# The last layer norm of a two-layer decoder trunk: g taken into the rows as they arrive, and one sum with b - mean * rstd * g

## The chip, the cores and the metric

The kernel runs on one core of one Trainium2 chip. The metric is the device time of one execution in microseconds; three timed runs of the kernel before gave a median of 2086.51 us. Engines are called PE (matmuls), DVE (VectorE), ACT (ScalarE), POOL (GpSimd) and SP (SyncE, which issues the DMAs).

## What is computed

Two post-norm decoder layers over 512 rows of 2048 channels in float32. Only the end of the second matters here: the mixed heads go through an output projection, the residual is added, and the last layer norm follows.

```python
def layer_norm(x, g, b):
    mean = jnp.mean(xf, axis=-1, keepdims=True)
    var = jnp.mean(jnp.square(xf - mean), axis=-1, keepdims=True)
    return ((xf - mean) * lax.rsqrt(var + LN_EPS) * g + b).astype(x.dtype)
...
    return o.astype(x.dtype) @ w_o                       # end of the second layer
...
    x = layer_norm(DEEPNORM_ALPHA * x + y, ln_g[layer], ln_b[layer])
```

## The kernel before, in words

Rows are cut into four slices of 128 rows, t0 to t3, which lie on the 128 partitions; channels run along the free axis. `proj_ln` makes the projection. A weight in float32 is split into a high and a low part (`split`: ACT copies the high part at L137, DVE subtracts at L141), and each product takes three matmuls (L506 to L508). The output columns come in groups: 0 to 511 (for this layer already made, and read back as `y`), 512, 1024, then 1536 to 1791. In these groups the four slices are worked on together. The last group, columns 1792 to 2047, has all its weights resident, so that PE finishes one slice after the other: the statistics of a slice are complete as soon as PE has left it, while PE works on the next.

After each group `evac` adds the residual to the matmul result for one slice (L457, DVE, PSUM and SBUF in, SBUF out, into the row buffer `s`), and takes statistics of 256 columns (L459, BN_STATS). After the last group of a slice DVE merges them (L495), and `rstd` is made of five small instructions: ACT's square root (L209), and L211, L214, L216, L220 on DVE. Then `after` normalizes the slice in `layer1_out`:

- DVE, columns 0 to 1023 (0 to 1791 for t3): `(s - mean) * g` at L1287, and later `s * rstd + b` at L1295, in pieces of 512 columns.
- ACT, POOL, the other columns: ACT makes `s * rstd - mean * rstd` (L1291, with `nmr` from L1289), POOL multiplies by g (L1292) and adds b (L1293).
- SP stores pieces of 512 columns (L1281). The residual pieces are loaded by SP too (L1276), into a pool of six buffers with the tag `xr`.

g and b lie in SBUF as `lng` and `lnb`, broadcast to all partitions; their loads (L1272) are issued ahead of the group that starts at column 1024. The order of the instructions on each engine is set when the program is built; each engine runs its own list in order and waits on semaphores. In the list of DVE the first instruction of a slice (L457) stands behind the last of the slice before.

Of the kernel before, what the change touches and what calls it, by code (L numbers as in the profile page):

```python
# [8 lines left out]
F32 = mybir.dt.float32  # L9
F32R = mybir.dt.float32r  # L10
I32 = mybir.dt.int32
AF = mybir.ActivationFunctionType
ALU = mybir.AluOpType
# [4 lines left out]
P = 128  # L18
S = 512
D = 2048  # L20
NK = D // P
NT = S // P
# [12 lines left out]
class Kernel:  # L35
# [402 lines left out]
                nc.scalar.activation(t, pm, AF.Copy, scale=hs[:, 2 * g + n:2 * g + n + 1])  # L438
                yield t

    def proj_ln(self, ctx, W, mixed, residual, after, first=None, start=None):

        nc, tc = self.nc, self.tc
        rp = ctx.enter_context(tc.tile_pool(name="wres", bufs=1))
        sp = ctx.enter_context(tc.tile_pool(name="lns", bufs=1))
        st = [sp.tile([P, D], F32, name=f"s{t}") for t in range(NT)]
        stats = [sp.tile([P, 8, 6], F32, name=f"st{t}") for t in range(NT)]

        def unit(c0, k0, nk, w, pool=None, bufs=None):
            return self.wunit(W[k0 * P:(k0 + nk) * P, c0:c0 + w].rearrange("(k p) n -> p k n", p=P),
                              nk, w, pool, bufs)

        def evac(t, c0, w, ps):
            sl = st[t][:, c0:c0 + w]
            nc.vector.scalar_tensor_tensor(sl, residual(t, c0, w), ALPHA, ps, ALU.mult, ALU.add)  # L457
            for j in range(c0, c0 + w, 256):
                nc.vector.bn_stats(stats[t][:, j // 256, :], st[t][:, j:j + 256])  # L459

        def mms(ps, t, k, w, kk):
            tk = slice(t * P, (t + 1) * P)
            self.mm3b(ps, mixed[k][:, 0, tk], mixed[k][:, 1, tk], w[0][:, kk, :], w[1][:, kk, :], k == 0, k == NK - 1)

        for c0, wd in ((0, 512), (512, 512), (1024, 512), (1536, 256)):
# [6 lines left out]
            for k0 in range(0, NK, nk):  # L472
                w = unit(c0, k0, nk, wd)
# [15 lines left out]
        for t in range(NT):  # L489
# [6 lines left out]
            rstd = lambda: self.rsqrt_eps(sp, mv[:, 1:2], LN_EPS, 1, f"ln{t}")  # L496
            g = after(t, st[t], mv[:, 0:1], rstd)
# [760 lines left out]
    def layer1_out(self, x1_d, mixed, y_d):  # L1258
        nc, tc, i = self.nc, self.tc, self.i
        with ExitStack() as ctx:  # L1260
            rp = ctx.enter_context(tc.tile_pool(name="res1", bufs=6))
            rp.tile([P, 112], F32, name="pad1", bufs=1)
            wp = ctx.enter_context(tc.tile_pool(name="wp1", bufs=2))
            bv = {}

            def start(c0):

                if c0 == 1024:
                    self.wp, self.ww = wp, 1024
                    for n, ap in (("g1", i["ln_g"][1:2]), ("b1", i["ln_b"][1:2])):  # L1270
                        t = bv[n] = rp.tile([P, D], F32, name="ln" + n, bufs=1)
                        nc.sync.dma_start(t, ap.to_broadcast([P, D]))  # L1272

            def residual(t, c0, w):
                r = rp.tile([P, 512], F32, tag="xr", name="xr")[:, :w]
                nc.sync.dma_start(r, x1_d[t * P:(t + 1) * P, c0:c0 + w])  # L1276
                return r

            def after(t, sf, mean, rstd):
                g, b = bv["g1"], bv["b1"]  # L1280
                out = lambda sl: nc.sync.dma_start(self.out[0, t * P:(t + 1) * P, sl], sf[:, sl])  # L1281
                rstd = rstd()
                cut = 1792 if t == NT - 1 else 1024
                dve = [slice(c, min(c + 512, cut)) for c in range(0, cut, 512)]
                rest = [slice(c, min(c + 512, D)) for c in range(cut, D, 512)]
                for sl in dve:
                    nc.vector.scalar_tensor_tensor(sf[:, sl], sf[:, sl], mean, g[:, sl], ALU.subtract, ALU.mult)  # L1287
                nmr = rp.tile([P, 1], F32, tag="nmr", name="nmr", bufs=2)
                nc.vector.scalar_tensor_tensor(nmr, mean, -1.0, rstd, ALU.mult, ALU.mult)  # L1289
                for sl in rest:  # L1290
                    nc.scalar.activation(sf[:, sl], sf[:, sl], AF.Identity, scale=rstd, bias=nmr)  # L1291
                    nc.gpsimd.tensor_mul(sf[:, sl], sf[:, sl], g[:, sl])  # L1292
                    nc.gpsimd.tensor_add(sf[:, sl], sf[:, sl], b[:, sl])  # L1293
                for sl in dve:
                    nc.vector.scalar_tensor_tensor(sf[:, sl], sf[:, sl], rstd, b[:, sl], ALU.mult, ALU.add)  # L1295
                    out(sl)
                for sl in rest:
                    out(sl)
                yield

            def first(t):
                y = rp.tile([P, 512], F32, tag="y", name="y", bufs=2)
                nc.sync.dma_start(y, y_d[t])
                return y

            self.proj_ln(ctx, i["od_w_o"][0], mixed, residual, after, first, start)


def build(tc, ins, out):
# [26 lines left out]
```

## Time and profile before

| | us |
|---|---|
| three timed runs | 2082.32, 2086.72, 2086.51 (median 2086.51) |
| the profiled execution, its own time | 2082.76 |
| span of its instructions | 2081.1 |
| PE busy | 2015.5 |
| DVE busy | 1281.4 |
| ACT busy | 960.2 |
| POOL busy | 282.9 |

The span is counted from the first instruction to the last; the time of the execution is a little longer. Times in the rows below are microseconds from the span's start. A row names the line of the source, the operation, and the tiles, as output<-inputs.

### The profile page before, as it was taken

What the parts mean: (1) busy time and instruction counts of PE and PEld (TensorE: products, weight loads), DVE (VectorE), ACT (ScalarE), POOL (GpSimd) and SP (SyncE); (2) the same over time, 40 slices, a digit from 0 to 9 for tenths busy, and PEclk for the clock granted to TensorE, in tenths of its full rate; (3) what the DMA queues carried; (4) which work ended last, traced back from release to release, by engine and by line L of the source; (5) the groups of instructions that cost most, each with busy time, mean ns of one, the idle gap of its engine ahead of it and who ended that gap; (6) DMA issues with size and microseconds to landing.
All of it is one profiled execution on the core that took longest, in us unless ns stands there. A gap on an engine that the chain in (4) does not pass through costs nothing. (4 is left out here: it accounts for less than half of the span.)

```text
span 2081.1 us, 33937 instructions
## 1 busy us (share of the span) xinstructions
PE 2015.5 (97%) x13091; PEld 1635.0 (79%) x13091; DVE 1281.4 (62%) x2572; ACT 960.2 (46%) x1687; POOL 282.9 (14%) x550
## 2 busy tenths in 40 slices
PE   8999999999999998999999999999999999989996
PEld 7888888888888897777878888876777777767786
DVE  4344345444433358666866676668788888876336
ACT  3345445323322138654645564454565555564221
POOL 0000000000000000234000000013444444410003
PEclk9999999999999999999999999999999999999998
DMA  5222222233333353465365556542223332332733
GB/s 195 92 81 81 81 81 66 86 97 99 99 111 112 117 167 125 143 179 175 118 212 194 177 174 218 197 164 67 81 84 108 108 108 84 101 113 97 245 104 111
DMA packets 214033, 262.99 MB, mean 126 GB/s; under 512 B 15768, under 2 KB 161776, under 8 KB 213104
## 3 DMA queue, kind: packets, MB, share of 16 engines
q1 hardware_dynamic: 213872, 260.83, 38.9%
q8 instruction: 103, 1.69, 0.3%
q14 instruction: 58, 0.48, 0.1%
HBM read 214.32 MB, written 46.47 MB: 125 GB/s over the span
## 5 line engine op out<-in xcount | busy, mean ns | idle before, releaser
L141 DVE TENSOR_TENSOR wlo<-wraw,whi 128x1024 fp32r<-128x1024 f32 (+1 forms) x268 | 314.7, 1177 | 464.3 <-ACT whi L137 455.9
L137 ACT CAST whi<-wraw 128x1024 fp32r<-128x1024 f32 (+1 forms) x324 | 302.9, 938 | 538.3 <-PE ga L146 299.6
L145 PE MATMUL ga<-mx,whi 128*128 128x512 f32 x768 | 299.8, 391 | 3.9 <-ACT mx L137 3.9
L146 PE MATMUL ga<-mx,whi 128*128 128x512 f32 x768 | 300.2, 391 | 2.1 <-DVE mx L141 2.1
L145 PE MATMUL ga<-x,whi 128*128 128x512 f32 x768 | 300.5, 391 | 1.0 <-ACT whi L137 1.0
L147 PE MATMUL ga<-mx,wlo 128*128 128x512 f32 x768 | 300.0, 391 | 0.0
L147 PE MATMUL ga<-x,wlo 128*128 128x512 f32 x768 | 299.4, 390 | 0.5 <-DVE wlo L141 0.5
L146 PE MATMUL ga<-x,whi 128*128 128x512 f32 x768 | 299.2, 390 | 0.0
L508 PE MATMUL gb<-wlo,mixed 128*128 128x512 f32 (+1 forms) x576 | 196.9, 343 | 1.8 <-DVE wlo L141 1.8
L506 PE MATMUL gb<-whi,mixed 128*128 128x512 f32 (+1 forms) x576 | 197.4, 343 | 1.1 <-DVE s L457 1.1
L507 PE MATMUL gb<-whi,mixed 128*128 128x512 f32 (+1 forms) x576 | 196.9, 342 | 0.0
L145 PEld LDWEIGHTS ga<-mx,whi 128*128 128x128 f32 x768 | 144.7, 188 | 36.6 <-ACT mx L137 4.1
L146 PEld LDWEIGHTS ga<-mx,whi 128*128 128x128 f32 x768 | 144.7, 188 | 33.7 <-DVE mx L141 2.8
L147 PEld LDWEIGHTS ga<-x,wlo 128*128 128x128 f32 x768 | 144.2, 188 | 31.2 <-DVE wlo L141 1.0
L147 PEld LDWEIGHTS ga<-mx,wlo 128*128 128x128 f32 x768 | 144.6, 188 | 30.5
L145 PEld LDWEIGHTS ga<-x,whi 128*128 128x128 f32 x768 | 144.2, 188 | 30.6 <-ACT whi L137 1.3
L146 PEld LDWEIGHTS ga<-x,whi 128*128 128x128 f32 x768 | 144.3, 188 | 29.1
L141 POOL TENSOR_TENSOR wlo<-wraw,whi 128x128 fp32r<-128x128 f32 x224 | 100.3, 478 | 222.1 <-ACT whi L137 196.7
L508 PEld LDWEIGHTS gb<-wlo,mixed 128*128 128x128 f32 x576 | 109.1, 190 | 15.8 <-DVE wlo L141 3.4
L506 PEld LDWEIGHTS gb<-whi,mixed 128*128 128x128 f32 x576 | 109.1, 190 | 15.3 <-DVE s L457 2.8
L507 PEld LDWEIGHTS gb<-whi,mixed 128*128 128x128 f32 x576 | 109.2, 190 | 12.3
L145 PE MATMUL vps<-mx,whi 128*128 128x512 f32 x256 | 113.4, 443 | 0.8 <-ACT vT L891 0.8
(333 smaller groups left out, 3345.4 us busy)
## 6 DMA issues: line engine op xcount, KB each, us to landing
wraw<-in_ev_w_in SPq DMA_DIRECT2D x96, 512.0 KB, 3.6
wraw<-in_ev_w_out SPq DMA_DIRECT2D x32, 512.0 KB, 3.6
wraw<-in_od_w_k SPq DMA_DIRECT2D x32, 512.0 KB, 4.7
wraw<-in_od_w_r SPq DMA_DIRECT2D x32, 512.0 KB, 3.4
wraw<-in_od_w_g SPq DMA_DIRECT2D x32, 512.0 KB, 3.8
wraw<-in_od_w_v SPq DMA_DIRECT2D x64, 256.0 KB, 2.7
ar_d<-pAR SPq DMA_DIRECT2D x16, 512.0 KB, 2.6
bk_d<-pBK SPq DMA_DIRECT2D x16, 512.0 KB, 3.3
```

The source lines that it names most:

```text
L137: self.nc.scalar.copy(hi, src)
L141: (eng or self.nc.vector).tensor_sub(lo[:, sl], src[:, sl], hi[:, sl].bitcast(F32))
L145: mm(ps, ah, bh, start=start, stop=False)
L146: mm(ps, ah, bl, start=False, stop=False)
L147: mm(ps, al, bh, start=False, stop=stop)
L506: mm(ps, ah, bh, start=start, stop=False)
L507: mm(ps, al, bh, start=False, stop=False)
L508: mm(ps, ah, bl, start=False, stop=stop)
```

## The change

The layer norm is written as `s * g * rstd + (b - mean * rstd * g)`. The product with g is taken out of `after`: `scaled`, a new call at the end of `evac`, multiplies a slice of `s` by g in place once its statistics are taken, on POOL, in pieces of 128 columns (columns 0 to 1535 with the group at 1024, then 1536 on and 1792 on); for the last columns of t3 DVE does it in one instruction. The second term, `tm`, is made per slice once `nmr = -mean * rstd` is there: for columns 0 to 1023 by DVE in one instruction per 512, for the others by ACT (g times nmr) and POOL (plus b, in pieces of 128). Four sums on DVE, `s * rstd + tm`, then finish the slice, each followed by its store. `tm` takes four buffers of the pool `xr`, which the residuals use too.

```diff
-    def proj_ln(self, ctx, W, mixed, residual, after, first=None, start=None):
+    def proj_ln(self, ctx, W, mixed, residual, after, first=None, start=None, scaled=None):
...
             for j in range(c0, c0 + w, 256):
                 nc.vector.bn_stats(stats[t][:, j // 256, :], st[t][:, j:j + 256])
+            if scaled:
+                scaled(t, c0, w, st[t])
...
             def after(t, sf, mean, rstd):
...
                 rstd = rstd()
-                cut = 1792 if t == NT - 1 else 1024
-                dve = [slice(c, min(c + 512, cut)) for c in range(0, cut, 512)]
-                rest = [slice(c, min(c + 512, D)) for c in range(cut, D, 512)]
-                for sl in dve:
-                    nc.vector.scalar_tensor_tensor(sf[:, sl], sf[:, sl], mean, g[:, sl], ALU.subtract, ALU.mult)
                 nmr = rp.tile([P, 1], F32, tag="nmr", name="nmr", bufs=2)
                 nc.vector.scalar_tensor_tensor(nmr, mean, -1.0, rstd, ALU.mult, ALU.mult)
-                for sl in rest:
-                    nc.scalar.activation(sf[:, sl], sf[:, sl], AF.Identity, scale=rstd, bias=nmr)
-                    nc.gpsimd.tensor_mul(sf[:, sl], sf[:, sl], g[:, sl])
-                    nc.gpsimd.tensor_add(sf[:, sl], sf[:, sl], b[:, sl])
-                for sl in dve:
-                    nc.vector.scalar_tensor_tensor(sf[:, sl], sf[:, sl], rstd, b[:, sl], ALU.mult, ALU.add)
-                    out(sl)
-                for sl in rest:
+                sls = [slice(c, c + 512) for c in range(0, D, 512)]
+                tm = [rp.tile([P, 512], F32, tag="xr", name="tm") for _ in sls]
+                for q in (2, 3):
+                    nc.scalar.activation(tm[q], g[:, sls[q]], AF.Copy, scale=nmr)
+                    for c in range(0, 512, P):
+                        nc.gpsimd.tensor_add(tm[q][:, c:c + P], tm[q][:, c:c + P], b[:, sls[q].start + c:sls[q].start + c + P])
+                for q in (0, 1):
+                    nc.vector.scalar_tensor_tensor(tm[q], g[:, sls[q]], nmr, b[:, sls[q]], ALU.mult, ALU.add)
+                for q, sl in enumerate(sls):
+                    nc.vector.scalar_tensor_tensor(sf[:, sl], sf[:, sl], rstd, tm[q], ALU.mult, ALU.add)
                     out(sl)
                 yield
+
+            def scaled(t, c0, w, sf):
+
+                if c0 < 1024:
+                    return
+                a = 0 if c0 == 1024 else c0
+                if c0 == 1792 and t == NT - 1:
+                    nc.vector.tensor_mul(sf[:, a:], sf[:, a:], bv["g1"][:, a:])
+                    return
+                for c in range(a, c0 + w, P):
+                    nc.gpsimd.tensor_mul(sf[:, c:c + P], sf[:, c:c + P], bv["g1"][:, c:c + P])
```

How the lists of the engines change, at three places. First DVE, slice t1 (its row buffer is `s_18599`; `s_18600` is that of t2), from the merged statistics to the first instruction of t2, before:

```order
L495 BN_AGGR mv<-st_18603 128x2 [waits DVE_49]
L211 TENSOR_SCALAR rshln_19610<-mv 128x1 [waits DVE_49]
L1287 SCALAR_TENSOR_TENSOR s_18599<-s_18599,mv,lng_18946 128x512
L214 RECIPROCAL rssln_19609<-rssln_19609 128x1 [waits Activation_49]
L1287 SCALAR_TENSOR_TENSOR s_18599<-s_18599,mv,lng_18946 128x512
L216 TENSOR_SCALAR rstln_19611<-rssln_19609,rshln_19610 128x1 [waits DVE_49]
L220 SCALAR_TENSOR_TENSOR rsyln_19612<-rstln_19611,rssln_19609 128x1 [waits DVE_49]
L1289 SCALAR_TENSOR_TENSOR nmr<-mv,rsyln_19612 128x1 [waits DVE_49]
L1295 SCALAR_TENSOR_TENSOR s_18599<-s_18599,rsyln_19612,lnb_18948 128x512 x2
L457 SCALAR_TENSOR_TENSOR s_18600<-xr,gb 128x256 [waits DMAHW7_49,PE_49]
```

Two products with g stand among the small instructions, two sums with b behind them, and nothing here waits for POOL. The same stretch of DVE with the change:

```order
L498 BN_AGGR mv<-st_18603 128x2 [waits DVE_49]
L211 TENSOR_SCALAR rshln_19680<-mv 128x1 [waits DVE_49]
L214 RECIPROCAL rssln_19679<-rssln_19679 128x1 [waits Activation_49]
L216 TENSOR_SCALAR rstln_19681<-rssln_19679,rshln_19680 128x1 [waits DVE_49]
L220 SCALAR_TENSOR_TENSOR rsyln_19682<-rstln_19681,rssln_19679 128x1 [waits DVE_49]
L1288 SCALAR_TENSOR_TENSOR nmr<-mv,rsyln_19682 128x1 [waits DVE_49]
L1296 SCALAR_TENSOR_TENSOR tm<-lng_18946,nmr,lnb_18948 128x512 [waits DVE_49]
L1296 SCALAR_TENSOR_TENSOR tm<-lng_18946,nmr,lnb_18948 128x512
L1298 SCALAR_TENSOR_TENSOR s_18599<-s_18599,rsyln_19682,tm 128x512 [waits DVE_49] x2
L1298 SCALAR_TENSOR_TENSOR s_18599<-s_18599,rsyln_19682,tm 128x512 [waits Activation_49,Pool_49] x2
L458 SCALAR_TENSOR_TENSOR s_18600<-xr,gb 128x256 [waits DMAHW3_49,PE_49]
```

The two L1287 ahead of `nmr` are gone, six instructions of 128x512 follow it, and the last two wait for POOL; the first instruction of t2 (L458, before L457) stands behind these.

Second POOL, slice t1 and the first row of t2, before:

```order
L1292 TENSOR_TENSOR s_18599<-s_18599,lng_18946 128x512 [waits Activation_49]
L1293 TENSOR_TENSOR s_18599<-s_18599,lnb_18948 128x512 [waits Pool_49]
L1292 TENSOR_TENSOR s_18599<-s_18599,lng_18946 128x512 [waits DVE_49,Activation_49]
L1293 TENSOR_TENSOR s_18599<-s_18599,lnb_18948 128x512 [waits Pool_49]
L1292 TENSOR_TENSOR s_18600<-s_18600,lng_18946 128x512 [waits Activation_49]
```

Two products and two sums of 512 columns. POOL, slice t1, with the change:

```order
L1311 TENSOR_TENSOR s_18599<-s_18599,lng_18946 128x128 [waits DVE_49]
L1311 TENSOR_TENSOR s_18599<-s_18599,lng_18946 128x128
L1294 TENSOR_TENSOR tm<-tm,lnb_18948 128x128 [waits DMAHW4_49,DMAHW1_49,Activation_49]
L1294 TENSOR_TENSOR tm<-tm,lnb_18948 128x128 x3
L1294 TENSOR_TENSOR tm<-tm,lnb_18948 128x128 [waits DMAHW7_49,DMAHW0_49,Activation_49]
L1294 TENSOR_TENSOR tm<-tm,lnb_18948 128x128 x3
```

They have become two products (L1311, columns 1792 on) and eight sums of 128 columns. The products of the earlier columns stand ahead of these in POOL's list: for each of the column ranges 0 to 511, 512 to 1023 and 1024 to 1535 four pieces of every slice, then two pieces of every slice for 1536 to 1791, 56 in all.

Third SP, from the last residual loads to the stores of t0 (`s_18598`) and t1, before:

```order
L1276 DMA xr<-x_d 128x256 [waits DMAHW7_49,DVE_49]
L1276 DMA xr<-x_d 128x256 [waits DMAHW0_49,DVE_49]
L1281 DMA out<-s_18598 128x512 [waits DMAHW1_49,DVE_49,Pool_49]
L1281 DMA out<-s_18598 128x512 [waits DMAHW2_49,DVE_49]
L1281 DMA out<-s_18598 128x512 [waits Pool_49] x2
L1281 DMA out<-s_18599 128x512 [waits DMAHW5_49,DVE_49]
L1281 DMA out<-s_18599 128x512 [waits DMAHW6_49,DVE_49]
```

All residual loads (L1276) stand ahead of the first store. SP with the change:

```order
L1279 DMA xr<-x_d 128x256 [waits DMAHW6_49,DMAHW0_49,DVE_49]
L1284 DMA out<-s_18598 128x512 [waits DMAHW7_49,DVE_49]
L1284 DMA out<-s_18598 128x512 [waits DVE_49]
L1284 DMA out<-s_18598 128x512 [waits DMAHW1_49,DVE_49]
L1284 DMA out<-s_18598 128x512 [waits DVE_49]
L1279 DMA xr<-x_d 128x256 [waits Activation_49,Pool_49]
L1284 DMA out<-s_18599 128x512 [waits DMAHW4_49,DVE_49]
```

The last residual of t2 (L1279) moved behind the four stores of t0, and that of t3 in the same way behind those of t1. The list of PE is the same in both.

## Rows read from the trace of the kernel before

**Rows 1.** The page's first part: busy time, share of the span and instructions of each engine.

```profile
PE 2015.5 (97%) x13091; PEld 1635.0 (79%) x13091; DVE 1281.4 (62%) x2572; ACT 960.2 (46%) x1687; POOL 282.9 (14%) x550
```

**Rows 2.** Busy time by stretches of the tail, cut where DVE starts the first instruction (L457) of t0, t1, t2 and t3 and where it ends: length, then PE, PEld, DVE, ACT, POOL busy with instruction counts, granted clock, DMA share, GB/s.

```profile
2047.67:2053.43 5.76, 5.76 (x50) 5.76 (x49) 4.59 (x12) 1.82 (x3) 1.34 (x1) 1.00 0.13 49
2053.43:2059.88 6.45, 6.45 (x56) 6.45 (x55) 6.27 (x12) 1.50 (x3) 5.16 (x5) 1.00 0.31 114
2059.88:2067.32 7.44, 5.03 (x42) 4.83 (x41) 7.27 (x13) 1.82 (x4) 6.14 (x5) 0.99 0.38 142
2067.32:2077.60 10.28, 0.00 (x0) 0.00 (x0) 10.18 (x17) 1.21 (x3) 7.97 (x6) 0.50 0.42 157
```

**Rows 3.** The chain of work that ended last, its end: start, length, engine, tile, line.

```profile
2055.64 1.63 DVE s L1287
...
2072.27 1.48 DVE s L1287
...
2075.61 1.99 DVE s L1295 x2
```

**Rows 4.** PE in order of time, its last matmul: start, length, engine, line, operation.

```profile
2064.63 0.28 PE L508 MATMUL gb<-wlo,mixed 128*128 128x256 f32 x1
```

**Rows 5.** DVE in order of time, slice t0: start, length, line, operation, output<-input shapes, count; in brackets idle time before it and what ended it.

```profile
2047.67 0.42 DVE L457 SCALAR_TENSOR_TENSOR s<-xr,gb 128x256 f32<-128x256 f32 x1 [4.88 <-PE gb L508]
2048.13 0.43 DVE L459 BATCH_NORM_STATS2 st<-s 128x6 f32<-128x256 f32 x1
2048.59 0.37 DVE L495 BATCH_NORM_AGGREGATE mv<-st 128x2 f32<-128x48 f32 x1
2049.00 0.15 DVE L211 TENSOR_SCALAR rshln<-mv 128x1 f32<-128x1 f32 x1
2049.07 0.74 DVE L1287 SCALAR_TENSOR_TENSOR s<-s,mv,lng 128x512 f32<-128x512 f32 x1
2049.73 0.16 DVE L214 RECIPROCAL rssln<-rssln 128x1 f32<-128x1 f32 x1
...
2050.45 0.27 DVE L216 TENSOR_SCALAR rstln<-rssln,rshln 128x1 f32<-128x1 f32 x1
2050.76 0.16 DVE L220 SCALAR_TENSOR_TENSOR rsyln<-rstln,rssln 128x1 f32<-128x1 f32 x1
2050.95 0.16 DVE L1289 SCALAR_TENSOR_TENSOR nmr<-mv,rsyln 128x1 f32<-128x1 f32 x1
2051.03 1.41 DVE L1295 SCALAR_TENSOR_TENSOR s<-s,rsyln,lnb 128x512 f32<-128x512 f32 x2
```

**Rows 6.** DVE in order of time, slice t2, the two products with g.

```profile
2061.27 1.78 DVE L1287 SCALAR_TENSOR_TENSOR s<-s,mv,lng 128x512 f32<-128x512 f32 x1
...
2063.04 1.70 DVE L1287 SCALAR_TENSOR_TENSOR s<-s,mv,lng 128x512 f32<-128x512 f32 x1
```

**Rows 7.** POOL in order of time, its first instructions in the tail and those beside rows 6.

```profile
2052.09 1.49 POOL L1292 TENSOR_TENSOR s<-s,lng 128x512 f32<-128x512 f32 x1 [191.51 <-ACT s L1291]
...
2061.20 1.30 POOL L1293 TENSOR_TENSOR s<-s,lnb 128x512 f32<-128x512 f32 x1
2062.46 1.74 POOL L1292 TENSOR_TENSOR s<-s,lng 128x512 f32<-128x512 f32 x1
```

**Rows 8.** DVE in order of time at two places of the middle of the second layer, instructions with two inputs in SBUF.

```profile
1428.61 0.60 DVE L962 TENSOR_TENSOR pr<-uc,la 128x169 f32<-128x169 f32 x1
...
1589.35 0.69 DVE L1109 SCALAR_TENSOR_TENSOR gm<-gm,ldg 128x512 f32<-128x512 f32 x1
```

**Rows 9.** POOL in order of time, pieces of 128 columns: two beside rows 8 and then an undisturbed run, its first piece alone and all four of it.

```profile
1428.98 0.55 POOL L141 TENSOR_TENSOR wlo<-wraw,whi 128x128 fp32r<-128x128 f32 x1
...
1589.64 0.70 POOL L141 TENSOR_TENSOR wlo<-wraw,whi 128x128 fp32r<-128x128 f32 x1 [2.37 <-ACT whi L137]
...
1699.07 0.46 POOL L141 TENSOR_TENSOR wlo<-wraw,whi 128x128 fp32r<-128x128 f32 x1 [5.40 <-ACT whi L137]
...
1699.07 1.71 POOL L141 TENSOR_TENSOR wlo<-wraw,whi 128x128 fp32r<-128x128 f32 x4 [5.40 <-ACT whi L137]
```

**Rows 10.** The group of columns 512 on: PE's last wait there and DVE's next preparation of a weight, in order of time; and PE's busy time and matmul count in the stretch of the group at 1024 (columns as in rows 2).

```profile
1950.81 0.50 PE L508 MATMUL gb<-wlo,mixed 128*128 128x512 f32 x1 [1.02 <-DVE wlo L141]
...
1954.56 0.69 DVE L141 TENSOR_TENSOR wlo<-wraw,whi 128x512 fp32r<-128x512 f32 x1 [2.55 <-ACT whi L137]
...
1973.00:2016.00 43.00, 43.00 (x192) 35.49 (x191) 14.23 (x20) 7.38 (x7) 0.00 (x0) 1.00 0.29 92
```

**Rows 11.** DVE in order of time, an instruction of 256 columns with both inputs in SBUF.

```profile
2073.74 0.47 DVE L1287 SCALAR_TENSOR_TENSOR s<-s,mv,lng 128x256 f32<-128x256 f32 x1
```

**Rows 12.** ACT in order of time, slice t0: the square root and the first scaled copy.

```profile
2049.00 0.29 ACT L209 ACTIVATE rssln<-mv,eps 128x1 f32<-128x1 f32 x1 [10.96 <-DVE mv L495]
...
2051.15 0.82 ACT L1291 ACTIVATE s<-s,nmr,rsyln 128x512 f32<-128x512 f32 x1 [1.85 <-DVE nmr L1289]
```

**Rows 13.** SP in order of time, the issue of the last store, and the summary of all stores: time from issue to landing.

```profile
2078.05 0.40 SPq L1281 DMA_DIRECT2D out<-s  x1
...
DMA to landing us min/median/max: 1.9/2.1/2.2
```

**Rows 14.** DMA issues by line, the residual pieces of 256 columns: count, KB each, median us from issue to landing.

```profile
xr<-x_d SPq DMA_DIRECT2D x8, 128.0 KB, 2.6
```

More of the change, by code (lines that the diff above doesn't have):

```diff
@@ L1304, in first @@
                 return y
-            self.proj_ln(ctx, i["od_w_o"][0], mixed, residual, after, first, start)
+            self.proj_ln(ctx, i["od_w_o"][0], mixed, residual, after, first, start, scaled)
 def build(tc, ins, out):
```

## The prediction

> **What bounds it now.** I read the engine shares first: PE is busy 97% of the span, so the kernel as a whole is matmul time, and the change touches no matmul [rows 1]. Then the stretches of the last 34 us [rows 2]. The final projection walks four row slices t0 to t3, and PE ends one every 5.76 us (first stretch). DVE begins t0 and t1 as PE delivers them, but t1 takes it 6.45 us, t2 7.44 us, and t3, with nothing left on PE, 10.28 us. So from t1 on the work behind the matmuls is the bound, and the chain of waits agrees: its last 26 us are DVE alone, line L1287 above all [rows 3]. PE's last matmul ends at 2064.91 [rows 4], DVE's last sum at 2077.60; only these 12.7 us, plus the landing of the output, are open to the change.
>
> Next, why DVE is slow there. Alone, a 128x512 sum of two SBUF tensors (L1287, L1295) takes 0.74 us, two in a row 1.41 [rows 5]. While POOL works, L1287 takes 1.70 to 1.78 and ends 0.54 to 0.55 us after the POOL instruction that was under way: 2061.20+1.30=2062.50 against 2063.05; 2062.46+1.74=2064.20 against 2064.74 [rows 6, 7]. The loser waits for the winner's whole instruction, then needs 0.54 more. POOL pays the same way: a 128x128 piece that started while DVE held the two-tensor form ends 0.32 us after DVE (1428.61+0.60=1429.21 against 1429.53), or 0.30 (1590.04 against 1590.34) [rows 8, 9]. Undisturbed pieces follow each other every (1.71-0.46)/3=0.42 us [rows 9].
>
> **What the change removes and adds in the tail** (L1292 to L1311 and L458 are its own line numbers; L458 is L457 of before). Removed per slice: two L1287 on DVE (four for t3) and four POOL instructions of 128x512, 1.3 to 1.8 us each [rows 7]. Added per slice: two L1296 on DVE, two scaled copies on ACT in place of two, eight 128x128 sums on POOL, and four last sums L1298 on DVE where two L1295 were (four for t3). DVE's 128x512 instructions so go from four to six for t0 to t2, and from eight (two of them 256 wide) to six for t3. The greater difference is the order: before, nothing on DVE waited for POOL's result; now the last two sums of each slice do, and DVE's own order puts the next slice's L458 behind them. POOL's chain comes in series with DVE's.
>
> **The multiplies by g.** 48+8 POOL pieces of 0.42 us move ahead of the tail. The order of POOL shows them in three batches of 16 and one of 8, each released by the statistics of one column range (the first also by the load of g). A batch of 16 takes 6.7 us, with one or two blocked pieces some 9, against 20 to 43 us from one range to the next (the group at 1024 is 43 us long) [rows 10]. The last 8 take 3.4 us, and the statistics that release them are done 4.88 us before t0 begins [rows 5]. None is left by then, and I cost them at nothing. Their neighbours are the two-tensor subtractions L141 that prepare the weights: each can wait for one piece, 0.42 at most. PE's last wait for such a weight ends at 1950.81; then the tightest is the L141 that ends at 1955.25 [rows 10]. A matmul takes 43/192=0.224 us there, a unit is 12 of them and needs its low half at the third, so PE comes to this one at 1950.81+(10+12+2)x0.224=1956.2, an estimate. That leaves 0.9 us for a wait of 0.42. If this cover were gone, PE would be late by what exceeds it. The last two pieces of a slice (1792 on) run behind BN_STATS beside BN_AGGR and the short instructions, which do not wait in these rows. For t3 DVE does that multiply itself: nearest row 0.47 for 128x256 [rows 11], less 0.07 of overlap, +0.4 us.
>
> **The new period T of a slice**, from the start of its first DVE instruction. Up to nmr: L457 0.42, BN_STATS and BN_AGGR bring L211 to 1.33 (2049.00-2047.67), ACT's root takes 0.29, and then L214, L216, L220, L1289 of 0.16, 0.27, 0.16, 0.16 with about 0.04 ahead of each: 2.52 [rows 5, 12]. Then:
> - DVE's L1296 twice: 0.04+1.41, to 3.97. ACT's first copy: 0.04+0.82, to 3.38; POOL can start 0.13 later (2051.97 to 2052.09 is 0.12), at 3.51 [rows 5, 7, 12], but finds DVE holding, so piece 1 ends at 3.97+0.32=4.29.
> - From here they alternate: first sum 0.54 (4.83), piece 2 0.32 (5.15), second sum 0.54 (5.69), piece 3 0.32 (6.01), piece 4 0.42 (6.43).
> - The third sum needs piece 4, but POOL has begun piece 5 before DVE learns of it: 0.42 (6.85), then 0.54 (7.39), piece 6 0.32, pieces 7 and 8 0.42 each (8.55).
> - The fourth sum needs piece 8: 0.04+0.74, to 9.33. The next slice's L458 starts 0.08 before that end: **T=9.25**.
>
> PE's 5.76 is faster, so DVE is never short of matmuls. Total: 3x9.25 + 9.33 + 0.4 = 37.48 us in place of 29.93 (5.76+6.45+7.44+10.28): +7.5. The end: before, two stores queued behind each other, the last issued at 2078.05, 0.45 after DVE's end [rows 13]; now one follows at once, of 256 KB and not 128, which lands 0.2 later (2.1 against 1.9): -0.2. **Sum +7.3 us.** SP's order also moves: the residuals of t2 and t3 are now issued behind the stores of t0 and t1. A residual lands 2.6 us after its issue [rows 14]; t0's last store is issued near 2057.0, t2 needs its residual near 2066.2, so 6 us are spare. The profiled execution took 2082.76, the median is 2086.51: 2090.1 by the one, 2093.8 by the other, and I give the latter.
>
> The price that no row shows as such is the alternation of four 128x128 pieces with 512-column sums. Below: pieces that DVE passes freely, T=3.51+7x0.42+0.46+0.04+0.74-0.08=7.6. Above: each side pays its full duration after the other, 0.74 for 0.54 three times and 0.42 for 0.32 four times, T=10.25. I take 9.25, because the nearest rows are the same forms, and in them the loser saves part of its duration [rows 6 to 9]. The Trainium skill ("SBUF — State Buffer", Who interferes with whom) says that whichever of the two issues first gets the shared pair of ports for the whole instruction and the other fully blocks. The trace agrees on the blocking (1.70 against 0.74), but by that rule taken to the letter, with full durations behind each other, the sum would be +11.3 and not +7.3.
>
> **Rivals.**
> - *The pieces slip past.* Small pieces leave gaps; L1109 kept 0.69 beside a piece, though there DVE had started first; against it speaks L962, stretched to 0.60 by a piece of this very size [rows 8, 9]. T=7.6: 3x7.6+7.7+0.4-29.93-0.2=+0.8, 2087.3: no change. Chance 0.18.
> - *Full hold.* Nothing is saved by the loser: +11.3, 2097.8. Chance 0.11. Against it: the 0.54 and 0.32 measured [rows 6 to 9]. The rule above is this case.
> - *The weights come late.* Four L141 near 1954 to 1962 wait for more than one piece each and use up the 0.9 us; PE then slips by up to 4x0.4: +8.9, 2095.4. Chance 0.04.
> - *The other side: the tail gets shorter.* POOL's new chain would have to be so quick that T falls below 7.41, where 4T+0.08+0.4-0.2 equals 29.93. With free passing and 0.32 per piece T=6.8: 3x6.8+6.85+0.4-29.93-0.2=-2.5, 2084.0. For it: POOL's four 128x512 per slice are gone from the tail. Against: a piece takes 0.42 even undisturbed [rows 9]. Chance 0.09, of which 0.05 would be read as faster.
> - That the change doesn't do what it says I exclude: the orders below the diff show the instructions.
>
> **How the numbers follow.** Forecast, alternation with T=9.25: chance 0.58, 2093.8. Range: from the free pass less the spread of the runs (2087.3-1.8) to the full hold, 2085.5 to 2098; outside lie most of the last rival and stray runs. About 0.2%, 4.2 us, is what a measurement of this kernel can tell. Slower 0.58+0.11+0.04=0.73; same 0.18+0.04=0.22; faster 0.05.
>
> **What would show it.** Starts of L458 for the four slices: 9.25 us apart by the forecast, 7.6 by the free pass, 10.25 by the full hold. In each slice the first two last sums (L1298) last over 0.8 us, the fourth starts when POOL's eighth piece ends. PE's end stays at 2064.9. The forecast is wrong if the steps are below 8 us, or if PE's end moves by more than 1 us.

## The result: 7.3 us more by the medians, and the steps of the last slices as forecast

The changed kernel takes 2093.19 us (median of 9 runs, 2090.84 to 2096.95) against 2085.89 us (9 runs, 2081.81 to 2087.46): +7.3. The ratio of the runs is 1.0043, 95% interval 1.0034 to 1.0052, that is +9.0 us (7.1 to 10.8). The profiled execution took 2092.6 us, its span is 2090.5; so 2.1 us of the execution lie outside the span, where it was 1.7 before (2082.76 less 2081.1).

The engines' shares, the page's first part, answer to [rows 1]:

```profile
PE 2019.1 (97%) x13091; PEld 1637.3 (78%) x13091; DVE 1280.5 (61%) x2577; ACT 961.1 (46%) x1688; POOL 308.8 (15%) x630
```

DVE's busy time is 0.9 us less than before (an instruction counts as busy while it stands behind POOL, too), and still the kernel is slower: the loss is not DVE's work, it is waiting between its instructions. The stretches of the tail, cut again where DVE starts the first instruction of t0 to t3 (columns as in [rows 2]):

```profile
2049.75:2059.02 9.27, 9.27 (x79) 9.27 (x78) 6.88 (x15) 1.63 (x3) 6.10 (x10) 1.00 0.23 85
2059.02:2068.27 9.25, 7.97 (x67) 7.76 (x65) 6.87 (x15) 1.64 (x3) 6.10 (x10) 1.00 0.39 129
2068.27:2077.46 9.19, 0.00 (x0) 0.00 (x0) 6.85 (x15) 1.63 (x3) 6.02 (x10) 0.69 0.39 128
2077.46:2087.07 9.61, 0.00 (x0) 0.00 (x0) 7.27 (x16) 1.63 (x3) 5.02 (x8) 0.50 0.29 109
```

The steps are 9.27, 9.25, 9.19 and 9.61, together 37.32 us (forecast 37.48), in place of 29.93. In the first three, DVE is busy only 6.9 of 9.2 us. Where it stands still is seen in DVE's slice t1 in order of time (compare [rows 5]):

```profile
2059.02 0.41 DVE L458 SCALAR_TENSOR_TENSOR s<-xr,gb 128x256 f32<-128x256 f32 x1
...
2061.36 0.16 DVE L1288 SCALAR_TENSOR_TENSOR nmr<-mv,rsyln 128x1 f32<-128x1 f32 x1
2061.56 1.41 DVE L1296 SCALAR_TENSOR_TENSOR tm<-lng,nmr,lnb 128x512 f32<-128x512 f32 x2
2062.89 1.82 DVE L1298 SCALAR_TENSOR_TENSOR s<-s,rsyln,tm 128x512 f32<-128x512 f32 x2
2065.49 0.94 DVE L1298 SCALAR_TENSOR_TENSOR s<-s,rsyln,tm 128x512 f32<-128x512 f32 x1 [0.78 <-POOL tm L1294]
2067.61 0.75 DVE L1298 SCALAR_TENSOR_TENSOR s<-s,rsyln,tm 128x512 f32<-128x512 f32 x1 [1.18 <-POOL tm L1294]
2068.27 0.41 DVE L458 SCALAR_TENSOR_TENSOR s<-xr,gb 128x256 f32<-128x256 f32 x1
```

and in POOL's and ACT's rows of the same slice:

```profile
2059.97 0.89 POOL L1311 TENSOR_TENSOR s<-s,lng 128x128 f32<-128x128 f32 x2 [1.66 <-DVE st L460]
2062.36 5.21 POOL L1294 TENSOR_TENSOR tm<-tm,lnb 128x128 f32<-128x128 f32 x8 [1.50 <-ACT tm L1292]
...
2061.56 1.34 ACT L1292 ACTIVATE tm<-lng,nmr 128x512 f32<-128x512 f32 x2 [0.93 <-DVE nmr L1288]
```

The third and fourth sums wait 0.78 and 1.18 us for POOL's pieces, and the eight pieces take 5.21 us where undisturbed ones would take 3.4 (7x0.42+0.46). The chain that ended last now runs through POOL, where before it was DVE alone [rows 3]. Its end, start and length:

```profile
2062.37 5.20 POOL tm L1294 x8
...
2072.50 4.26 POOL tm L1294 x7
...
2082.92 3.38 POOL tm L1294 x6
```

PE's last matmul begins 2.08 us later than in [rows 4], and so do the last slices (2049.75 against 2047.67):

```profile
2066.71 0.28 PE L511 MATMUL gb<-wlo,mixed 128*128 128x256 f32 x1
```

The span's +9.4 us are therefore +7.39 of the tail, +2.08 ahead of it, and -0.07 behind it. The 2.08 were not forecast; the section on e4_early takes them apart.

### The profile page after: what moved, and what is told of

Read it like the earlier page. It is cut to its first block, busy times and chain, and to the rows that moved or that the text cites. A ratio compares the mean times of both kernels' runs of the same rounds, so it can differ in the third digit from the quotient of the medians.

```text
span 2090.5 us, 34040 instructions
## 1 busy us (share of the span) xinstructions
PE 2019.1 (97%) x13091; PEld 1637.3 (78%) x13091; DVE 1280.5 (61%) x2577; ACT 961.1 (46%) x1688; POOL 308.8 (15%) x630
## 5 line engine op out<-in xcount | busy, mean ns | idle before, releaser
L141 DVE TENSOR_TENSOR wlo<-wraw,whi 128x1024 fp32r<-128x1024 f32 (+1 forms) x268 | 314.1, 1175 | 464.6 <-ACT whi L137 459.7
L141 POOL TENSOR_TENSOR wlo<-wraw,whi 128x128 fp32r<-128x128 f32 x224 | 100.1, 478 | 221.4 <-ACT whi L137 192.2
```

The source lines that it names most:

```text
L141: (eng or self.nc.vector).tensor_sub(lo[:, sl], src[:, sl], hi[:, sl].bitcast(F32))
```

## The experiments

The tail's steps are told as start to start of the four slices and to the end of DVE's last sum. Differences of time are the ratio's, with its 95% interval.

| kernel | steps, us | tail | against the kernel before: tail | time |
|---|---|---|---|---|
| before | 5.76, 6.45, 7.44, 10.28 | 29.92 | | |
| changed | 9.27, 9.25, 9.19, 9.61 | 37.32 | +7.4 | +9.0 (7.1 to 10.8) |
| e1_defer | 5.65, 8.55, 7.72, 10.67 | 32.60 | +2.7 | +4.4 (2.5 to 6.5) |
| e2_piece512 | 8.62, 8.60, 8.53, 8.95 | 34.70 | +4.8 | +6.5 (3.8 to 9.2) |
| e3_alldve | 7.85, 7.86, 7.85, 8.27 | 31.82 | +1.9 | +1.5 (-0.4 to 3.5) |
| e6_psumtm | 8.37, 8.36, 8.29, 8.72 | 33.74 | +3.8 | +5.4 (3.1 to 7.5) |
| e4_early | 5.76, 6.45, 7.44, 10.28 | 29.93 | 0.0 | 0.0 (-2.1 to 2.1) |
| e7_psumgb | 5.60, 5.60, 5.60, 8.16 | 24.96 | -5.0 | -4.2 (-6.0 to -2.3) |
| e8_psumgb_small | 5.65, 5.65, 5.65, 8.05 | 25.01 | -4.9 | -4.8 (-6.7 to -3.1) |
| e10_late | 5.76, 6.44, 7.44, 10.28 | 29.92 | 0.0 | -0.4 (-2.1 to 1.5) |
| e9_psumgb_late | 5.60, 5.60, 5.60, 8.10 | 24.90 | -5.0 | -4.0 (-5.6 to -2.1) |

### e1_defer: the series of DVE and POOL undone

```diff
...
+                bv["nmr"], r2 = nmr, rstd
                 for q, sl in enumerate(sls):
-                    nc.vector.scalar_tensor_tensor(sf[:, sl], sf[:, sl], rstd, tm[q], ALU.mult, ALU.add)
+                    if q == 2:
+                        yield
+                        if t < NT - 1:
+                            r2 = rp.tile([P, 1], F32, tag="r2", name="r2", bufs=2)
+                            nc.vector.scalar_tensor_tensor(r2, bv["nmr"], 0.0, rstd, ALU.mult, ALU.add)
+                    nc.vector.scalar_tensor_tensor(sf[:, sl], sf[:, sl], r2 if q > 1 else rstd, tm[q], ALU.mult, ALU.add)
                     out(sl)
-                yield
```

(The third and fourth sums take `r2`, which equals rstd but depends on the next slice's `nmr`; the first two `tm` of a slice lie in the buffers `y`, so that the pool suffices.)

> The changed kernel, but the third and fourth sums of a slice stand on VectorE behind the next slice's statistics and its mean*rstd term, so that they no longer wait for GpSimd's pieces. Nothing is left out. Theory (the slice is a chain: statistics, product on ScalarE, four pieces on GpSimd twice, then the sum): the two idle gaps on VectorE of 0.8 and 1.2 us in each slice go, and with them the period of 9.2; the slices start 5.8 (t0, which hands two sums on), then 7.3 to 7.5 apart, the last takes about 10.6 with six sums in it; total from the first evacuation to the end of the last sum about 31, against 37.3 of the changed kernel and 29.9 of the one before. The time then falls by about 6 us from the changed kernel's 2093. Rival (VectorE's own work, and what GpSimd's pieces add to it, sets the period and not the waiting): 9.2 stays, total 37, no change of the time.

Measured: 2086.44 us (median of 10; 2084.21 for the kernel before, 24 runs), tail 32.60: 4.7 us less than the changed kernel, not the 6.3 expected. DVE, the end of slice t1, in order of time:

```profile
2055.05 1.81 DVE L1297 SCALAR_TENSOR_TENSOR tm<-lng,nmr,lnb 128x512 f32<-128x512 f32 x2
2056.79 1.82 DVE L1305 SCALAR_TENSOR_TENSOR s<-s,rsyln,tm 128x512 f32<-128x512 f32 x2
2058.53 0.41 DVE L1304 SCALAR_TENSOR_TENSOR r<-nmr,rsyln 128x1 f32<-128x1 f32 x1
2059.04 1.71 DVE L1305 SCALAR_TENSOR_TENSOR s<-s,r,tm 128x512 f32<-128x512 f32 x2
```

In t0 to t2 no wait is left ahead of a sum, so the waits were the series, as the theory says; t3, with no slice behind it, keeps two (0.43 and 0.34 us). But in t1 POOL is now at work beside all six long instructions, each pair takes 1.7 to 1.8 in place of 1.41, and even the 128x1 ones grow (0.41 for 0.16). The steps are 8.55 and 7.72, not 7.4: the rival was right to the extent that work beside POOL is dearer, which I had counted for the two middle sums alone. The gain is mostly t0's, which hands two sums on (5.65).

### e2_piece512: one sum of 512 columns on POOL

```diff
-                    for c in range(0, 512, P):
-                        nc.gpsimd.tensor_add(tm[q][:, c:c + P], tm[q][:, c:c + P], b[:, sls[q].start + c:sls[q].start + c + P])
+                    nc.gpsimd.tensor_add(tm[q], tm[q], b[:, sls[q]])
```

> The changed kernel, but GpSimd adds b in one instruction of 512 columns instead of four of 128. Nothing is left out. Theory (GpSimd's pieces are dear because each alternates with a VectorE instruction and starts anew: 0.9 each beside VectorE, 0.45 alone, eight of them 5.0 us): two adds at 1.3 to 1.5 alone and less alternation, period 8.6 instead of 9.2, total about 34.9, 2.4 us less than the changed kernel. Rival (small pieces spare VectorE: it never stands behind a GpSimd instruction for over 0.3 us; a long one makes it stand for all of its 1.2): the first two sums become 1.7 instead of 0.95, the period 9.7 to 11, total 39 to 44.

Measured: 2089.08 us (5 runs), step 8.60 and tail 34.70, by the theory (8.6 and 34.9). DVE's sums in slice t1, the first alone and the next two, and POOL's two instructions:

```profile
2061.88 1.79 DVE L1297 SCALAR_TENSOR_TENSOR s<-s,rsyln,tm 128x512 f32<-128x512 f32 x1
...
2063.59 2.44 DVE L1297 SCALAR_TENSOR_TENSOR s<-s,rsyln,tm 128x512 f32<-128x512 f32 x2
```
```profile
2061.36 1.77 POOL L1293 TENSOR_TENSOR tm<-tm,lnb 128x512 f32<-128x512 f32 x1 [1.51 <-ACT tm L1292]
...
2063.08 1.74 POOL L1293 TENSOR_TENSOR tm<-tm,lnb 128x512 f32<-128x512 f32 x1
```

The rival's dear sums are there, 1.79 us for the first and 1.77 for the second; the first ends 0.54 after POOL's instruction (2061.36+1.77=2063.13 against 2063.67), as in [rows 6]. POOL's two also come out dearer than the theory had them, 1.77 and 1.74 us and not 1.3 to 1.5. Both cost less than they look, because DVE would have waited for POOL anyway, and POOL is done sooner: where four pieces took four turns, one instruction takes one, and the two end 6.80 us after the slice's start (2063.08+1.74-2058.02), against 8.55 for the eight pieces. Splitting POOL's work into 128 columns makes each of DVE's sums cheaper (0.94 for 1.79), but it gives POOL more turns to wait, and DVE waits for POOL.

### e3_alldve: DVE makes all of tm

```diff
-                for q in (2, 3):
-                    nc.scalar.activation(tm[q], g[:, sls[q]], AF.Copy, scale=nmr)
-                    for c in range(0, 512, P):
-                        nc.gpsimd.tensor_add(tm[q][:, c:c + P], tm[q][:, c:c + P], b[:, sls[q].start + c:sls[q].start + c + P])
-                for q in (0, 1):
+                for q in range(4):
```

> The changed kernel, but VectorE makes all four pieces of b - mean*rstd*g itself; ScalarE makes none and GpSimd adds nothing in the last four slices. Nothing is left out. Theory (the chain over ScalarE and GpSimd and its alternation with VectorE cost more than the work that they take off VectorE): no idle gaps, sums and products at their undisturbed 0.74 to 0.75; 4 more instructions' worth at 0.75 are 2 of them new (1.5 us), the gaps of 0.8 and 1.2 and the 0.2 twice and 0.18 go; period about 7.9 for the first three slices, the last about 8.3, total about 32, 5.4 us less than the changed kernel. Rival (VectorE's work sets the period): 1.5 us a slice more, period 10.7, total 43.

Measured: 2085.87 us (10 runs), steps 7.85, tail 31.82, by the theory (7.9 and 32). DVE in slice t1, eight long instructions one behind the other, all undisturbed:

```profile
2058.26 2.74 DVE L1292 SCALAR_TENSOR_TENSOR tm<-lng,nmr,lnb 128x512 f32<-128x512 f32 x4
2060.92 2.73 DVE L1294 SCALAR_TENSOR_TENSOR s<-s,rsyln,tm 128x512 f32<-128x512 f32 x4
```

Giving two of the eight long instructions to ACT and POOL cost 1.4 us a slice more than keeping them on DVE (9.25 against 7.85).

### e6_psumtm: the first two pieces of tm in PSUM

```diff
+            pm = ctx.enter_context(tc.tile_pool(name="ptm", bufs=1, space=PSUM))
...
-                tm = [rp.tile([P, 512], F32, tag="xr", name="tm") for _ in sls]
+                tm = [pm.tile([P, 512], F32, tag="tm", name="tm", bufs=4) if q < 2 else
+                      rp.tile([P, 512], F32, tag="xr", name="tm") for q in range(4)]
```

> The changed kernel, but VectorE writes its two pieces of b - mean*rstd*g to PSUM, so that the first two sums read one operand from SBUF and one from PSUM. Nothing is left out. Theory (an instruction of VectorE that takes two operands from SBUF alternates with GpSimd's pieces, one that takes one does not): the first two sums fall from 0.95 to 0.7, GpSimd's pieces beside them from 0.9 to 0.46, so GpSimd's chain ends 1.4 us a slice earlier; period about 8.4, total about 33.9, 3.4 us less than the changed kernel. Rival (any VectorE instruction alternates with GpSimd, wherever its operands lie, or the pieces are slow for another reason): sums 0.95, pieces 0.9, period 9.2, no change.

Measured: 2089.56 us (8 runs), step 8.36, tail 33.74, by the theory (8.4 and 33.9). Slice t1, DVE's first two sums with `tm` in PSUM and the third with `tm` in SBUF; then POOL's eight pieces and two of them, beside the first sums, alone:

```profile
2060.49 1.40 DVE L1300 SCALAR_TENSOR_TENSOR s<-s,rsyln,tm 128x512 f32<-128x512 f32 x2
2062.19 0.93 DVE L1300 SCALAR_TENSOR_TENSOR s<-s,rsyln,tm 128x512 f32<-128x512 f32 x1 [0.30 <-POOL tm L1296]
```
```profile
2059.96 4.32 POOL L1296 TENSOR_TENSOR tm<-tm,lnb 128x128 f32<-128x128 f32 x8 [1.50 <-DMA xr<-x_d]
...
2060.86 0.88 POOL L1296 TENSOR_TENSOR tm<-tm,lnb 128x128 f32<-128x128 f32 x2
```

Beside the same pieces the two sums with one operand from SBUF take 1.40 us together, as long as two undisturbed ones (1.41 [rows 5]), where the changed kernel's two, with both operands from SBUF, take 1.82; and the pieces beside them are undisturbed (0.88 for two, where two of L1311 took 0.89). The contention is one of SBUF operands, not of engines. The Trainium skill ("SBUF — State Buffer", Who interferes with whom) says that a DVE instruction with at most one SBUF input, outside its two-port modes, does not contend with GpSimd; these rows agree.

### e7_psumgb and e8_psumgb_small: the same remedy in the kernel before

```diff
+            pm = ctx.enter_context(tc.tile_pool(name="pgb", bufs=1, space=PSUM))
...
+                if c0 == 1536 and t == 0:
+                    one = rp.tile([P, 1], F32, name="one", bufs=1)
+                    nc.vector.tensor_scalar(one, sf[:, c0:c0 + 1], 0.0, 1.0, ALU.mult, ALU.add)
+                    for n in ("g1", "b1"):
+                        d = bv[n + "p"] = pm.tile([P, 1024], F32, name=n + "p")
+                        for c in (0, 512):
+                            nc.scalar.activation(d[:, c:c + 512], bv[n][:, c:c + 512], AF.Copy, scale=one)
...
+                at = lambda n, sl: bv[n + "p" if sl.stop <= 1024 else n][:, sl]
-                    nc.vector.scalar_tensor_tensor(sf[:, sl], sf[:, sl], mean, g[:, sl], ALU.subtract, ALU.mult)
+                    nc.vector.scalar_tensor_tensor(sf[:, sl], sf[:, sl], mean, at("g1", sl), ALU.subtract, ALU.mult)
```

(The sum with b likewise. `one` is 1.0 and only holds the copies back until the fourth column group, where ACT has time: they run from 2040.52 to 2043.05.) In e8 in addition:

```diff
-                nc.vector.scalar_tensor_tensor(nmr, mean, -1.0, rstd, ALU.mult, ALU.mult)
+                nc.vector.tensor_scalar(nmr, mean, -1.0, rstd, ALU.mult, ALU.mult)
```

and in the same way the instruction of L220.

> The kernel before, with g and b of columns 0 to 1023 copied to PSUM by ScalarE ahead of the last slices, so that VectorE's first and second operations on these columns read one operand from SBUF. Nothing is left out. Theory (an operation of VectorE with two SBUF operands stands behind GpSimd's instruction for all that is left of it, 1.78 and 1.70 instead of 0.74; with one it passes): the contended operations fall to about 0.75, and with them the steps of 6.45, 7.44 and 10.28; total from the first evacuation to the last sum about 26.2 against 29.9, 3.7 us less than before. Rival (VectorE stands behind GpSimd wherever its operands lie): steps as before, total 29.9, no change.

> As the run with g and b in PSUM, and the two small operations (128x1) that end the statistics take their second factor as a per-partition scalar instead of a tensor. Nothing is left out. Theory (these too take two SBUF tensors and stand behind GpSimd when it is busy): another 0.6 us, total about 25.6, 4.3 us less than before. Rival (a 128x1 operation never stands there, or the scalar is read in the same way): no difference from the run with g and b in PSUM alone.

Measured: 2080.17 us (12 runs) and 2079.51 us (12 runs), the kernel before 2083.39 (29 runs): ratios 0.9980 (0.9971 to 0.9989) and 0.9977 (0.9968 to 0.9985). Both are faster than either kernel. The stretches of e7, cut as above:

```profile
2047.50:2053.10 5.60, 5.60 (x50) 5.60 (x49) 4.57 (x12) 1.82 (x3) 1.19 (x1) 1.00 0.11 41
2053.10:2058.70 5.60, 5.60 (x50) 5.60 (x49) 5.42 (x12) 1.54 (x3) 4.30 (x5) 1.00 0.39 143
2058.70:2064.30 5.60, 5.57 (x48) 5.37 (x46) 4.94 (x13) 2.10 (x4) 5.45 (x5) 1.00 0.40 146
2064.30:2072.46 8.16, 0.00 (x0) 0.00 (x0) 8.05 (x16) 0.89 (x2) 6.45 (x6) 0.72 0.60 222
```

DVE in slice t1 of e7, POOL beside it, and one row of e8:

```profile
2053.10 0.42 DVE L457 SCALAR_TENSOR_TENSOR s<-xr,gb 128x256 f32<-128x256 f32 x1 [0.86 <-PE gb L510]
...
2054.50 0.74 DVE L1291 SCALAR_TENSOR_TENSOR s<-s,mv,g1p 128x512 f32<-128x512 f32 x1
2055.23 0.72 DVE L1291 SCALAR_TENSOR_TENSOR s<-s,mv,g1p 128x512 f32<-128x512 f32 x1
...
2056.18 1.05 DVE L220 SCALAR_TENSOR_TENSOR rsyln<-rstln,rssln 128x1 f32<-128x1 f32 x1
```
```profile
2054.54 1.30 POOL L1296 TENSOR_TENSOR s<-s,lng 128x512 f32<-128x512 f32 x1
2055.91 1.29 POOL L1297 TENSOR_TENSOR s<-s,lnb 128x512 f32<-128x512 f32 x1
```
```profile
2056.47 0.21 DVE L221 TENSOR_SCALAR rsyln<-rstln,rssln 128x1 f32<-128x1 f32 x1
```

The products run beside POOL's instruction at 0.74 and 0.72 where they took 1.78 and 1.70 [rows 6], and POOL's take 1.30 and 1.29, where one beside DVE's took 1.74 [rows 7]. The steps fell further than expected (5.60, total 24.96 instead of 26.2), down to PE's own pace: DVE waits 0.86 us for PE at the start of t1 and 0.49 at that of t3, so PE sets the steps again. That is also why e8 does not gain the further 0.6 us that were expected: its small instruction did fall from 1.05 to 0.21, but off the path that sets the end; only the last slice shows it (8.16 to 8.05).

Not all of the 5.0 us is the operands' doing. PE's 48 matmuls of a slice took 5.60 us in e7 and e9 and 5.65 in e8 and e1, but 5.76 in the kernel before, all at a granted clock of 1.00. With 5.76 the three steps of e7 would be 0.5 us longer, which leaves some 4.5 for the operands. What sets this pace is not shown; in the group at 1024 it went the other way (0.233 us from matmul to matmul in e7 to e9, 0.227 in the kernel before).

### e4_early: the products with g alone, ahead of the tail

```diff
...
+            def scaled(t, c0, w, sf):
+                if c0 < 1024 or c0 == 1792:
+                    return
+                a = 0 if c0 == 1024 else c0
+                scr = rp.tile([P, 512], F32, tag="y", name="scr", bufs=2)
+                for c in range(a, c0 + w, P):
+                    nc.gpsimd.tensor_mul(scr[:, :P], sf[:, c:c + P], bv["g1"][:, c:c + P])
...
```

> The kernel before, with GpSimd's 56 early products of 128 columns added (48 after the third column block, 8 after the 512 columns behind it), written to a tile that nobody reads. The last norm is as before. Theory (they lie beside PE's work and touch nothing that PE waits for; the later start of the last slices in the profile of the changed kernel was the wait for a residual that landed late, which comes in either kernel): time equal to that of the kernel before within 0.1%, first evacuation of the last slices at 2047.7, or 2049.8 with the same wait of PE near 1951 of some 1.8 us and the lower clock behind it, which then must show in a kernel without these products too. Rival (the products slow VectorE's share of the weights, or GpSimd stands in front of something): PE waits for a weight between 1952 and 2016, the first evacuation of the last slices 1 to 2 us later in each profile, time 1 to 2 us more than before.

Measured: 2084.19 us (11 runs) against 2083.39, ratio 1.0000 (0.9990 to 1.0010); the tail is that of before to 0.01 us. In the profile the last slices start at 2049.01, with the late wait of PE. In the changed kernel first, DVE's and PE's rows at this place, and the stretches behind PE's wait:

```profile
1950.09 0.69 DVE L458 SCALAR_TENSOR_TENSOR s<-xr,y 128x512 f32<-128x512 f32 x1 [2.94 <-DMA xr<-x_d]
...
1951.44 0.50 PE L511 MATMUL gb<-wlo,mixed 128*128 128x512 f32 x1 [1.84 <-DVE wlo L141]
...
1952.80 7.68 POOL L1311 TENSOR_TENSOR s<-s,lng 128x128 f32<-128x128 f32 x16 [93.10 <-DVE wlo L141]
```
```profile
1951.44:1953.50 2.06, 2.06 (x7) 1.64 (x8) 1.20 (x3) 0.00 (x0) 0.70 (x2) 0.70 0.44 138
1953.50:1956.00 2.50, 2.50 (x8) 1.98 (x7) 0.34 (x1) 0.62 (x1) 2.50 (x7) 0.57 0.92 358
```

and in e4 the same:

```profile
1949.31 0.69 DVE L457 SCALAR_TENSOR_TENSOR s<-xr,y 128x512 f32<-128x512 f32 x1 [3.54 <-DMA xr<-x_d]
...
1950.66 0.50 PE L510 MATMUL gb<-wlo,mixed 128*128 128x512 f32 x1 [2.44 <-DVE wlo L141]
```
```profile
1950.66:1953.00 2.34, 2.34 (x7) 1.80 (x7) 1.20 (x3) 0.00 (x0) 0.69 (x2) 0.60 0.59 179
1953.00:1956.00 3.00, 3.00 (x11) 2.44 (x10) 0.69 (x1) 0.62 (x1) 3.00 (x7) 0.74 0.90 362
```

DVE stands for a residual, the weight's low half (L141) stands behind it, PE stands for that; then the granted clock is 0.57 to 0.74 on average, so that PE ran for much of the stretch at the lower of its two levels, 1.2 GHz. In the changed kernel the wait is over 1.4 us ahead of POOL's first product (1952.80), so the products did not make it. Where the products do run beside the L141 that prepare the later weights, these take up to 0.94 us in place of 0.69, but in the changed kernel PE waits for none of them.

### e10_late and e9_psumgb_late: the load of g moved away from that residual

```diff
                 if c0 == 1024:
                     self.wp, self.ww = wp, 1024
+                if c0 == 1536:
                     for n, ap in (("g1", i["ln_g"][1:2]), ("b1", i["ln_b"][1:2])):
```

> The kernel before, with the loads of g and b (1 MB each on the chip) issued at the start of the fourth column block instead of the third. Nothing is left out. Theory (the wait of PE near 1951, 1.0 us in the profile of before and 1.8 in that of the changed kernel, comes from a residual that is issued 0.4 us ahead of the load of g and lands 5.5 to 6.9 us after its issue; this wait, and the lower clock that can follow, make the spread of the last slices' start): without the load beside it the residual lands some 3 us after its issue, as its neighbours do (2.6 to 3.5), the evacuation of the fourth slice's first block starts 2 to 3 us after its residual's issue at the latest, PE's waits near 1947 and 1951 fall below 0.5 us together, the last slices start 1 to 2 us earlier, tail 29.9 as before; time 1 to 2 us less than before. Rival (the wait is for the weights, the load only stands beside it): waits of PE as before, no change, or worse where g now meets the weights of the fourth block.

> The run with g and b of columns 0 to 1023 in PSUM and the two small operations with a scalar, and the loads of g and b at the start of the fourth column block. Nothing is left out. Theory: both gains add, the tail at 25.0 as there and the last slices 1 to 2 us earlier; 5 to 7 us less than the kernel before. Rival (the loads meet the weights of the fourth block or come late for ScalarE's copies): tail 25.0 again, but the last slices at the same time or later; 3 to 5 us less than before.

Measured: 2083.41 us (12 runs; before 2083.84, 23 runs), ratio 0.9998 (0.9990 to 1.0007), and 2079.63 us (12 runs), ratio 0.9981 (0.9973 to 0.9990). No gain over the kernels without the move: this theory fell. In e10 PE waits once, 0.90 us; in e9 DVE again stands 2.25 us for the residual with no load of g beside it:

```profile
1949.91 0.69 DVE L460 SCALAR_TENSOR_TENSOR s<-xr,y 128x512 f32<-128x512 f32 x1 [2.25 <-DMA xr<-x_d]
```

What makes the residual late is open. That the changed kernel's work makes it late is not shown. From the issue of the first of SP's four stores of `y` to the start of t0, with the waits of PE (over 0.1 us) in between, in the eleven profiles:

| | without the early products | with them |
|---|---|---|
| from store to t0, us | 119.7, 120.1, 120.6, 121.3, 121.4 | 120.5, 120.6, 121.6, 122.0, 122.6, 123.1 |
| less PE's waits | 118.8, 118.2, 118.3, 119.1, 118.9 | 118.1, 118.1, 118.9, 119.6, 119.5, 119.8 |

Without the waits, the two groups lie at 118.6 and 119.0 on average. The three highest, 119.5 to 119.8, are e4, e6 and the changed kernel, which have the longest single waits of all (2.44, 1.79 and 1.84 us); behind these the granted clock fell, and in the other eight profiles it stayed at 1.00 there. In e6:

```profile
1952.00:1954.50 2.50, 2.50 (x7) 1.93 (x7) 0.61 (x1) 0.62 (x1) 1.68 (x4) 0.50 0.93 306
```

So the 2.08 us by which the changed kernel's last slices start later come apart like this: it reached the store 0.91 us sooner than the kernel before (1926.68 against 1927.59), its PE waited 1.45 us longer (3.29 against 1.84), and the other 1.54 are about what the low clock costs: an estimate from the two stretches of the changed kernel above, 30% of 2.06 us and 43% of 2.50, is 1.7.

The waits differ from profile to profile in both groups, and average 2.0 us without the early products and 2.7 with them. (In e1 and e2, 0.6 us of them is a wait for a weight near 1966 and 1969, beside no piece of POOL.) Whether the change makes them longer is more than one profile of each kernel can tell. The timed ratios leave room for it: the changed kernel, e1, e2 and e6 lie 1.6 to 1.7 us above what their tails account for, each with an interval of some 2 us either way, and the four kernels without the early products between 0.4 below and 1.0 above. Against it, e3 lies 0.4 us below, and e4, which has the early products alone, measured 0.0.

## Why the prediction was right, step by step

- **What bounds the kernel, and that only the tail is open to the change:** held for the tail, which gave +7.39 of the span's +9.4; whether the +2.08 ahead of it has to do with the change is open. (The chain before is DVE alone for its last 24.2 us, from 2053.43, not 26.)
- **The sum, +7.3 us:** the tail and its end measured +7.32. That the two medians differ by the same 7.3 is luck in part: the ratio of the runs gives +9.0 (7.1 to 10.8), the profile's span +9.4, and the 2.08 us ahead of the tail stood in no term of the sum.
- **The period T=9.25:** 9.27, 9.25 and 9.19. Its parts: `nmr` ready 2.52 after the start, measured 2.50 (2061.36+0.16-2059.02); DVE's two L1296 end at 3.97, measured 3.95 (2061.56+1.41-2059.02). The pieces of POOL end at 8.55, measured 2062.36+5.21-2059.02=8.55. The fourth sum starts as POOL's eighth piece ends (2067.57 against 2067.61) and takes 0.75. The first two sums last 0.95 each, "over 0.8" as said.
- **The price of the alternation** (the unknown of the sum): the value taken, 0.54 and 0.32 for the loser, was right; e2 shows 0.54 again. "The pieces slip past" (7.6) and "Full hold" (10.25) are both excluded by the steps. With full durations behind each other the sum would have been 4.0 us too dear (+11.3 against +7.32): here the loser saves 0.2 of its 0.74. The rule of the Trainium skill that the prediction cites ("SBUF — State Buffer", Who interferes with whom) was right on who contends; that the other fully blocks stands there of DVE's two-port modes, and of an instruction with two SBUF inputs it says only that it contends.
- **t3:** +0.4 for its own product with g, measured 0.42 (9.61-9.19). The sum of the tail was 0.16 too high (37.48 against 37.32), mostly from the last step.
- **The short instructions "do not wait in these rows":** a reading from t0 of the kernel before, where POOL stood still. Beside POOL they do wait (L220 took 0.95 us in its t1). Here it cost nothing, because POOL's two products end at 2060.86, ahead of L220, and its first sum starts behind `nmr`.
- **The end:** -0.2 forecast, -0.07 measured in the profile's span behind DVE's end: the term that was mis-sized, by 0.13 us.
- **The multiplies by g cost nothing:** e4 agrees as far as its interval goes, 0.0 us (-2.1 to 2.1). In the changed kernel the three batches of 16 take 6.8 to 7.8 us, and the last 8 end 3.9 us before t0 begins.
- **"PE's end stays at 2064.9":** missed. It came at 2066.99, 2.08 us later, and by the prediction's own sign (over 1 us) this step is wrong. The rival "The weights come late" named another place, 1954 to 1962, and another mechanism, L141 waiting for POOL's pieces; the runs show a wait at 1951, for a residual, ahead of any piece, and a low clock behind it, and the wait varies in profiles without the products too. Why the residual is late is open. I had taken the single profile of before as free of such spread.
- **SP's moved residuals:** DVE's first instruction of t2 and of t3 waits for no residual, as said.

The prediction saw that DVE stands behind POOL in the kernel before, but not what that costs as a whole. e7 answers it: some 4.5 us of its tail were DVE and POOL standing behind each other for SBUF. The change took POOL's long instructions out, and put POOL's short ones in series with DVE instead.

## What to carry to other kernels

When two engines share a resource, count the turns: splitting the helper's work into small pieces makes more of them, and if the main engine needs the helper's result, each turn is on the path. First ask which operand makes the instructions collide, and move that (here g and b to PSUM, -4.2 us in e7), before moving the work. And a last phase that hangs on a chain over three engines is read by its idle gaps, not by its busy time: here DVE's busy time fell by 0.9 us while the tail grew by 7.4.

## What the runs showed of the chip beyond what was expected

- Instructions of 128x1 wait too. With two tensors in SBUF, L220 took 0.95 us in the kernel before's slice t1 (the row below) and 1.05 in e7, for 0.16 alone; with its second factor as a per-partition scalar it took 0.21, beside the same instruction of POOL and with POOL idle.

```profile
2057.49 0.95 DVE L220 SCALAR_TENSOR_TENSOR rsyln<-rstln,rssln 128x1 f32<-128x1 f32 x1
```

- ACT's scaled copy without a bias takes 0.72 us for 128x512 (1.34 for two), the one with scale and bias 0.82 [rows 12]; the prediction took 0.82 for both, which cost nothing, since POOL's first piece waited for DVE. The Trainium skill ("ScalarE: Activation LUTs", What ACT_TABLE_LOAD costs) states some 93 ns for each per-partition operand; the 0.10 here agrees.
- Behind PE's wait of 1.84 us in the changed kernel the granted clock was 0.70 and then 0.57 over the next 4.6 us, behind that of 2.44 us in e4 it was 0.60 and then 0.74 over the next 5.3; behind the 1.02 us of [rows 10] it stayed at 1.00.
